# The up projection's products with both parts of x in one, its halves added afterwards, and the large sums in whole PSUM banks

## The chip, the cores and the metric

The kernel runs on one core of a Trainium2 chip. Times are device microseconds of one execution. The engines of the core are TensorE (PE), VectorE (DVE), ScalarE (ACT), GpSimd (POOL) and SyncE (SP), which here only issues DMAs. PE takes its weights from SBUF and writes to PSUM, which has eight banks of 128 partitions by 512 float32.

## The reference

A decoder trunk of two layers, batch 1, 256 positions, width 1024. In each layer four token mixers (stick-breaking, MoBA, NSA and differential attention) read one normalised input through one combined projection, their heads go through one output projection, and a squared-ReLU MLP of width 4096 follows. Cut to the layer:

```python
h = _rmsnorm(x, g_attn) @ w_in          # columns for four mixers
...
x = x + concat(heads) @ w_out
h = _rmsnorm(x, g_mlp)
x = x + square(relu(h @ w_up)) @ w_down
```

All values are float32.

## The kernel before

**Split products.** PE runs on float32r operands, which keep fewer bits than float32. Every operand of a weight product is therefore split into a high part and a rest (`whi` and `wlo`, `xh` and `xl`), and a product is the sum of three: high by high, low by high, high by low.

**Weights.** `Weights.load` brings a piece of 1 MB by a DMA on SP's queue into one of three `wraw` buffers. `Weights.part` makes the parts of each half of it: a copy on ACT gives `whi`, a subtraction on DVE `wlo` (four buffers each).

**Stages.** Per layer: `make_xT` transposes the normalised input; `attention` runs the projections group by group (`proj`: nqk, dqk, v2, mqk and others) and the mixers. `stack2` and `stack3` copy high and low parts of q and k (`qth`, `qtl`) from SBUF to SBUF by DMA into stacked tiles `s`, from which PE multiplies. `out_proj` sums the mixers' outputs (`mixh`, `mixl`) into `xs`. `mlp` transposes `xs`, and then runs 16 steps j: `up(j)` makes 256 rows of the hidden layer in one bank (two halves c2 of 128 rows by 256 positions), `down(j)` multiplies them by 256 rows of `w_down` and adds to sums that stay in PSUM over all j. In these sums the positions 0 to 127 (t=0) have two banks of 512 columns, and the positions 128 to 255 (t=1) one of 512 and two of 256 (`COLS`). The last two steps are done for t=0 first and then for t=1 (`late`).

**Order.** No instruction is issued as the code stands. All calls are recorded by a class `Order` with a clock (`at(...)`) and a price (`estimate`); a planner in the kernel then lists them by engine, takes buffers in that order, and issues them all from line 480. Fitted numbers shift the clocks: `START` for the mixers, `LOADS` for each piece's DMA, `LEADS` for the splits of its two halves, `FIRST` for the first transposes. So the order on every engine follows from tables, and a profile shows line 480 for all instructions; they are told apart by tiles.

Of the kernel before, what the change touches and what calls it, by code (L numbers as in the profile page):

```python
# [12 lines left out]
F32R = mybir.dt.float32r  # L13
# [11 lines left out]


START = {
    "sb": ((-1631.0, -246.3, -1469.7, 37.9), (-336.5, -802.8, -1167.9, 39.0)),
    "ns": ((24.7, -323.7, 51.7, 46.8), (48.1, -2091.9, 33.2, -513.6)),
    "cw": ((-1012.1,), (-1225.6,)),  # L30
    "cmp": ((-1143.8,), (-699.5,)),
    "df": ((-1505.4, -3076.6, -190.3, -1781.3), (-197.6, -1526.0, 53.3, 53.2)),
    "mb": ((-87.3, -375.0, -116.4, -375.3), (-1.8, -2266.1, -671.0, -7307.1)),
}

LOADS = (
    68.7, 29.2, 31.5, 51.3, 36.6, 20.0, 9.5, 12.4, 16.0, 18.7, 5.9, -3.0, 18.2, 25.0, 9.2, 6.3, 9.8, 11.4, -1.0,
    5.9, 21.8, 16.3, 17.8, 21.2, 19.9, 9.4, 20.0, 28.0, 19.8, 57.0, 26.1, 16.7, 48.9, 47.5, 12.4, 23.6, 0.7,
    34.2, 5.7, 44.0, 32.9, -9.7, -8.9, 50.3, 22.2, -0.2, 6.8, 5.6, 0.9, -15.7, 0.8, -1.0, 4.1, 12.3, 66.9, 11.7,
    21.0, 16.2, 19.5, 31.7, 16.4, 17.0, 2.2, 12.0, 15.5, 15.1, 15.5, 13.6, 7.0, 16.3, 10.4, 18.4, 18.9, 20.8,  # L40
    21.3, 38.5, 24.3, 35.9, 32.5, 35.0, 33.8, 38.0, 46.7, 46.1, 47.8, 42.4, -17.5, -43.3, -6.2, -47.0, -44.6,
    13.0, -98.1, 36.7, -17.0, 34.6, -186.6, -325.1, -520.8, -515.7, -829.1, -710.6, -2010.0, -2229.8,
)
LEADS = (
    (1347.0, 1199.9), (447.4, -513.5), (64.3, -1296.8), (1425.7, -228.5), (402.9, 87.1), (-2158.5, -31.4),
    (839.9, -708.1), (-442.8, 12.3), (5.0, -626.1), (457.2, -904.8), (23.6, 168.0), (245.1, -23.4), (74.1,
    15.0), (-742.0, -1243.8), (58.0, 77.0), (1958.8, 764.3), (68.0, 13.6), (2096.1, -632.8), (2366.8, 130.1),
    (885.9, 1.2), (646.0, 1.8), (12.9, -159.3), (-49.0, -121.0), (184.2, -17.1), (-126.7, -132.0), (988.3,
    399.4), (-372.6, -122.0), (-889.2, -1143.9), (-385.3, 112.3), (-169.7, -173.7), (3720.5, 160.6), (105.5,
    -789.1), (9.0, -138.6), (-21.2, -86.2), (307.3, -224.7), (1594.1, -229.4), (1624.4, 170.5), (-373.4, -90.2),  # L50
    (2213.6, -146.9), (-339.3, -784.8), (10.4, -954.9), (294.1, -57.0), (-93.3, 390.2), (152.5, 861.9), (1066.0,
    -1138.6), (123.6, 103.7), (-262.8, 1079.8), (545.5, -358.4), (167.1, 53.0), (215.8, 25.4), (237.4, 151.2),
    (2475.3, 5.0), (128.5, 166.4), (5.5, -36.6), (-395.1, -2225.0), (287.4, 385.8), (531.1, 940.7), (-329.1,
    386.5), (734.3, -564.9), (-121.7, -18.9), (564.5, -133.0), (252.0, 915.1), (39.9, 58.8), (34.0, -137.6),
    (-10.2, 275.5), (-292.3, -270.3), (184.7, 735.6), (1151.9, -34.2), (97.3, -1061.7), (-258.8, -1815.8),
    (259.4, 1814.3), (-47.6, 99.1), (1018.5, -2.8), (14.1, -3.1), (-1842.0, -958.3), (-136.1, -1227.7), (1.3,
    701.1), (585.0, -1068.1), (-1562.1, 1231.2), (24.5, 1607.1), (2827.1, 264.2), (608.5, -1576.0), (645.4,
    -597.8), (-122.1, 1895.3), (7.0, -329.3), (-340.0, -236.2), (-44.0, 156.5), (560.7, 294.5), (-130.7, 45.0),
    (420.1, -402.0), (-1157.7, -49.7), (2460.9, 615.7), (-445.7, -55.1), (-619.0, -2270.5), (-1175.0, -2091.0),
    (50.3, 974.9), (-18.5, 11.3), (299.0, 430.5), (25.8, 3068.0), (102.4, 1306.4), (511.2, 369.9), (-1495.2,  # L60
    181.7), (-385.3, -386.4), (-40.4, -107.4),
)
CW_LOAD = 41.5
STAGE = 1.2

FIRST = (-124.6, -741.4)
LAYER = 300.0
TINY = 1e-30
NEG = -1e30
# [108 lines left out]
class Order:  # L178
# [33 lines left out]
    def estimate(op, eng, method, writes, reads):  # L212
        o, n = writes[0], _columns_of(writes[0])
        if method == "dma_start":
            op.bytes = 4 * n * o.ap[0][1]
            if _space(o) == SBUF != _space(reads[0]) and "scratch" in reads[0].tensor.name and o.ap[0][1] < 64:
                op.bytes *= DMA_RATE / SLOW_RATE
            return 650.0 if _space(o) == _space(reads[0]) == SBUF else 475.0
        if eng == "PE":
# [264 lines left out]
def trunk(ctx: ExitStack, tc: tile.TileContext, x, w_in, w_out, w_up, w_down, gattn, gains, pos, cw1, cw2,  # L484
          lamv, subln, table, fnorm, eye, cst, hot, rows, out, order):
    nc = order
# [171 lines left out]

    def make_xT(src, gi=None):

        xh = ap.tile([128, 2, 8, 128], F32R, name="xh", tag="xh", bufs=1)
        xl = ap.tile([128, 2, 8, 128], F32R, name="xl", tag="xl", bufs=1)
        for t in range(2):
            if gi == 0:
                at(FIRST[t])
            for k4 in range(2):
# [11 lines left out]
                for i, k in enumerate(ks):  # L678
                    nc.vector.scalar_tensor_tensor(xl[:, t, k], p[:, i * 128:(i + 1) * 128], gn[:, gi, k:k + 1],
                                                   F(xh[:, t, k]), op0=ALU.mult, op1=ALU.subtract)  # L680
        return xh, xl


    COLS = (((0, 512), (512, 1024)), ((0, 512), (512, 768), (768, 1024)))

# [503 lines left out]
    VCs = []  # L1189

    def ps_out():
        return [[ps_acc() for _ in COLS[t]] for t in range(2)]

    def mms(acc, lhs, w, first, last, ts=(0, 1)):

        for t in ts:
            sl = slice(t * 128, (t + 1) * 128)
            for a, (c0, c1) in zip(acc[t], COLS[t]):
                o = a[:, :c1 - c0]
                for i, ((h, lo), (wh, wl)) in enumerate(zip(lhs, w)):  # L1200
                    mm(o, h[:, sl], wh[:, c0:c1], first and i == 0, False)
                    mm(o, h[:, sl], wl[:, c0:c1], False, False)
                    mm(o, lo[:, sl], wh[:, c0:c1], False, last and i == len(lhs) - 1)

    def out_proj(l, mix, clock):
        at(clock)
        acc = ps_out()
        late, ws = [], []
        order = [("sb", 0), ("ns", 2), ("df", 3), ("mb", 1)]
        for n, (name, idx) in enumerate(order):  # L1210
            w = Weights(w_out[l, idx], 2048, 2)
            m = mix[name].mix
            if n < 3:
                for i in range(2):
                    mms(acc, [m[i]], [w.part(i, clock)], n == 0 and i == 0, False)
                    clock += 2.6
            else:
                late += m
                ws += [w.part(i, clock + 2.6 * i) for i in range(2)]
                clock += 5.2  # L1220
        clock -= 5.2
        at(clock)
        mms(acc, late, ws, False, True, ts=(0,))
        at(clock, 2.6)
        mms(acc, late, ws, False, True, ts=(1,))
        at(clock, -4.0)
        for t in range(2):
            for a, (c0, c1) in zip(acc[t], COLS[t]):
                nc.vector.tensor_add(xs[:, t, c0:c1], a[:, :c1 - c0], xs[:, t, c0:c1])
        clock += 5.2  # L1230
        return clock + 5.2

    def mlp(l, clock):
        at(clock, -8.0)
        xh, xl = make_xT([xs[:, t] for t in range(2)], l + 1)
        at(clock, 10.0)
        r2 = [small(1), small(1)]
        for t in range(2):
# [2 lines left out]

        def up(j, clock):
            at(clock)
            p = ps_att()
            w = Weights(w_up[l, j], 2048, 2)
            hl = [w.part(c2, clock + 2.6 * c2) for c2 in range(2)]
            for c2, kh in (((0, 0), (1, 0), (0, 1), (1, 1)) if j == 0 else ((0, 0), (0, 1), (1, 0), (1, 1))):
                at(clock)
                hi, lo = hl[c2]
                o = p[:, c2 * 256:(c2 + 1) * 256]  # L1250
                for m, (a, x) in enumerate(((hi, xh), (lo, xh), (hi, xl))):
                    for k in range(4 * kh, 4 * kh + 4):
                        mm(o.rearrange("p (t c) -> p t c", t=2), a[:, k * 128:(k + 1) * 128], x[:, :, k], c2 == 0 and k == 0 and m == 0, k == 7 and m == 2)
                clock += 1.3
            at(clock)
            r, s = t2(), t2()
            nc.scalar.activation(r, p, AF.Relu)
            nc.vector.scalar_tensor_tensor(s, p, 0.0, r, op0=ALU.max, op1=ALU.mult)
            hh, hl = t2(F32R), t2(F32R)
            split(hh, hl, s)  # L1260
            return hh, hl
# [9 lines left out]
        for j in range(16):  # L1271
# [4 lines left out]
            at(c1)  # L1276
            if j < 14:
                for i in range(2):
                    mms(acc, lhs[i:i + 1], ws[i:i + 1], j == 0 and i == 0, False)
            else:  # L1280
                late.append((lhs, ws))
            h = nxt
        for t in range(2):
            for i, (lhs, ws) in enumerate(late):
                at(clock, 160.0 + 5.2 * t + 2.6 * i)
                mms(acc, lhs, ws, False, i == 1, ts=(t,))
        for t in range(2):
            for a, (c0, c1) in zip(acc[t], COLS[t]):
                nc.vector.scalar_tensor_tensor(xs[:, t, c0:c1], a[:, :c1 - c0], r2[t], xs[:, t, c0:c1],
                                               op0=ALU.mult, op1=ALU.add)  # L1290

    for l in range(DEPTH):
        at(l * LAYER, -12.0)
# [69 lines left out]
```

## Time and profile before

| | |
|---|---|
| median of three runs | 654.37 us (653.43 to 656.68) |
| the profiled execution | 658.14 us |
| its span, first to last instruction | 656.3 us |
| mean granted clock of PE in it | 0.990 |

The profile is one execution. Its span is what the views cut into stretches; 1.8 us lie around it. A clock of 1.00 is 2.4 GHz, 0.50 is 1.2 GHz.

### The profile page before, as it was taken

The page shows a single profiled execution, that of the slowest core. Times are in us where ns is not written, and L with a number is a line of the kernel's source. Part 1 is how long each engine was busy: PE and PEld are TensorE (multiplying, and loading weights), DVE is VectorE, ACT ScalarE, POOL GpSimd, SP SyncE. Part 2 cuts the span into 40 slices and gives each one's busy share as a digit, 9 for nine tenths or more (in the row PEclk, how much of TensorE's full clock was granted, in tenths as well). Part 3 has the DMA queues.
Part 4 walks back from the last instruction along what each step waited for, and adds up shares of the span by engine and source line. Part 5 has one row for each costly group of instructions (what it writes and reads, how often), then busy time and mean ns, then how long its engine had stood idle before and what let it go on. Part 6 is the DMA issues. An engine that isn't in the chain of part 4 may idle for free.

```text
span 656.3 us, 11070 instructions
## 1 busy us (share of the span) xinstructions
PE 632.1 (96%) x4390; PEld 570.7 (87%) x4390; DVE 413.1 (63%) x818; ACT 360.5 (55%) x675; POOL 8.1 (1%) x25
## 2 busy tenths in 40 slices
PE   5999999999999999999999999989999999999996
PEld 5988668789999999899889987877999999998995
DVE  6668479767536465554685585885865554655555
ACT  5556468567435445444364695866654454454443
POOL 1100000000000000000000000000000000000000
PEclk9999979999999999999999999998999999999999
DMA  7786935933645554457546977466245545545531
GB/s 295 276 258 183 268 157 207 275 129 129 212 174 193 193 191 148 174 193 257 180 143 209 276 256 194 194 192 205 100 177 205 202 172 193 193 160 193 193 129 64
DMA packets 26900, 127.02 MB, mean 194 GB/s; under 512 B 3880, under 2 KB 5928, under 8 KB 14048
## 3 DMA queue, kind: packets, MB, share of 16 engines
q1 hardware_dynamic: 26848, 126.32, 56.7%
q8 instruction: 34, 0.56, 0.3%
q14 instruction: 18, 0.15, 0.1%
HBM read 115.79 MB, written 3.17 MB: 181 GB/s over the span
## 4 chain that ended last, share of the span: by engine, by line
PE 77%; DMA 8%; DVE 6%; ACT 5%; SPq 2%; issue 1%; POOLq 0%; POOL 0%; ACTq 0%
PE ps L480 77%; ACT t L480 3%; DVE wlo L480 2%; DMA s<-qth 2%; DMA wraw<-in_w_in_dram 2%; SPq L480 2%; ACT whi L480 2%; DVE t L480 1%; DMA st<-parts_scratch 1%; DMA s<-qtl 1%; DMA wraw<-in_w_down_dram 1%; DVE xl L480 1%; DMA parts_scratch<-qth 1%; DVE sm L480 1%; DVE xs L480 1%
## 5 line engine op out<-in xcount | busy, mean ns | idle before, releaser
L480 DVE TENSOR_TENSOR wlo<-wraw,whi 128x1024 fp32r<-128x1024 f32 (+1 forms) x192 | 231.2, 1212 | 144.9 <-ACT whi L480 144.4
L480 ACT ACTIVATE whi<-wraw 128x1024 fp32r<-128x1024 f32 (+1 forms) x192 | 200.9, 1051 | 182.9 <-PE ps L480 143.1
L480 PE MATMUL ps<-whi,t 128*128 128x512 f32 (+1 forms) x640 | 169.1, 348 | 0.0
L480 PEld LDWEIGHTS ps<-whi,t 128*128 128x128 f32 x640 | 113.5, 189 | 16.3
L480 PE MATMUL ps<-xh,whi 128*128 128x256 f32 x768 | 122.6, 285 | 0.6 <-ACT whi L480 0.6
L480 PE MATMUL ps<-xl,whi 128*128 128x256 f32 x768 | 122.3, 284 | 0.0
L480 PE MATMUL ps<-xh,wlo 128*128 128x256 f32 x768 | 121.9, 284 | 0.0
L480 PE MATMUL ps<-wlo,t 128*128 128x512 f32 (+1 forms) x320 | 111.4, 349 | 0.6 <-DVE wlo L480 0.6
L480 PEld LDWEIGHTS ps<-xh,whi 128*128 128x128 f32 x768 | 105.0, 191 | 3.1 <-issue 1.4
L480 PEld LDWEIGHTS ps<-xl,whi 128*128 128x128 f32 x768 | 105.0, 191 | 0.3 <-issue 0.3
L480 PEld LDWEIGHTS ps<-xh,wlo 128*128 128x128 f32 x768 | 104.7, 192 | 0.4 <-issue 0.2
L480 PEld LDWEIGHTS ps<-wlo,t 128*128 128x128 f32 x320 | 60.6, 189 | 8.6 <-DVE wlo L480 0.9
L480 ACT ACTIVATE t<-ps 128x384 f32<-128x384 f32 (+3 forms) x79 | 40.0, 515 | 43.4 <-PE ps L480 43.0
L480 ACT ACTIVATE t<-t,sm 128x256 f32<-128x256 f32 (+1 forms) x110 | 47.2, 445 | 9.5 <-DVE sm L480 9.1
L480 DVE SCALAR_TENSOR_TENSOR t<-ps,t 128x512 f32<-128x512 f32 (+1 forms) x40 | 26.3, 660 | 23.7 <-ACT t L480 20.2
L480 DVE TENSOR_TENSOR t<-t,t 128x512 fp32r<-128x512 f32 (+2 forms) x44 | 27.4, 623 | 19.9 <-ACT t L480 19.2
L480 ACT ACTIVATE t<-t 128x512 fp32r<-128x512 f32 (+5 forms) x53 | 28.9, 548 | 14.6 <-DVE t L480 14.2
L480 DVE CUSTOM_DVE_ANT_0 t<-ps,Bt 128x256 f32<-128x256 f32 (+1 forms) x80 | 24.4, 352 | 10.9 <-PE ps L480 10.8
L480 PE MATMUL ps<-whi,mixh 128*128 128x512 f32 (+1 forms) x80 | 29.5, 370 | 0.0
L480 PE MATMUL ps<-wlo,mixh 128*128 128x512 f32 (+1 forms) x80 | 28.6, 358 | 0.0
L480 PE MATMUL ps<-whi,mixl 128*128 128x512 f32 (+1 forms) x80 | 28.5, 358 | 0.0
L480 PE MATMUL ps<-whi,xh 128*128 128x396 f32 (+1 forms) x64 | 20.7, 398 | 0.3 <-ACT xh L480 0.3
(143 smaller groups left out, 518.7 us busy)
## 6 DMA issues: line engine op xcount, KB each, us to landing
wraw<-in_w_up_dram SPq DMA_DIRECT2D x32, 1024.0 KB, 4.8
wraw<-in_w_down_dram SPq DMA_DIRECT2D x32, 1024.0 KB, 4.8
wraw<-in_w_in_dram SPq DMA_DIRECT2D x20, 1024.0 KB, 4.9
wraw<-in_cw_dram SPq DMA_DIRECT2D x8, 1024.0 KB, 5.3
wraw<-in_w_out_dram SPq DMA_DIRECT2D x8, 1024.0 KB, 6.7
s<-qth SPq DMA_DIRECT2D x28, 128.0 KB, 3.7
s<-qtl SPq DMA_DIRECT2D x28, 128.0 KB, 2.4
wraw<-in_w_in_dram SPq DMA_DIRECT2D x4, 792.0 KB, 5.5
```

What stands on the lines that cost most here:

```text
L480: fn(*a, **k)
```

## The change

It has four parts. In `up`, the parts of x stand in one tile `x4`, so that for each k the 256 columns of `xh` and the 256 of `xl` lie side by side; the high weights multiply all 512 in one product, and the low weights the 256 of `xh`. Each half c2 has a bank to itself, whose first 256 columns hold high by high and low by high, and the others high by low. ACT copies the latter to SBUF (`c`), DVE adds the former (`s`), and the squared ReLU is taken from `s`. In the sums, t=1 has two banks of 512 (`FULL`) except in the late part, which `finish` puts in one of these and two fresh banks of 256; the second bank is added to `xs` by itself. The planner's price for DMAs from SBUF to SBUF on up to 64 partitions rises. And all tables have new numbers.

```diff
 START = {
-    "sb": ((-1631.0, -246.3, -1469.7, 37.9), (-336.5, -802.8, -1167.9, 39.0)),
+    "sb": ((-2128.1, -135.2, -1435.8, 37.9), (-286.7, -731.7, -641.4, 39.7)),
...
 LOADS = (
-    68.7, 29.2, 31.5, 51.3, 36.6, 20.0, 9.5, 12.4, 16.0, 18.7, 5.9, -3.0, 18.2, 25.0, 9.2, 6.3, 9.8, 11.4, -1.0,
+    73.4, 61.3, 61.1, 82.6, 43.8, 72.8, 7.3, 8.2, 12.4, 12.9, 12.9, 2.7, 12.4, 54.6, 14.0, 10.8, 14.3, 8.1, 7.0,
...
-            if _space(o) == SBUF != _space(reads[0]) and "scratch" in reads[0].tensor.name and o.ap[0][1] < 64:
+            if _space(o) == SBUF and (_space(reads[0]) == SBUF or "scratch" in reads[0].tensor.name) and o.ap[0][1] <= 64:
                 op.bytes *= DMA_RATE / SLOW_RATE
...
-        xh = ap.tile([128, 2, 8, 128], F32R, name="xh", tag="xh", bufs=1)
-        xl = ap.tile([128, 2, 8, 128], F32R, name="xl", tag="xl", bufs=1)
+        x4 = ap.tile([128, 4096], F32R, name="x4", tag="x4", bufs=1)
+        if gi:
+
+            x4 = x4.rearrange("p (k m t c) -> p m t k c", k=8, m=2, t=2)
+        else:
+            x4 = x4.rearrange("p (m t k c) -> p m t k c", m=2, t=2, k=8)
+        xh, xl = x4[:, 0], x4[:, 1]
...
+    FULL = ((0, 512), (512, 1024))
...
-        return [[ps_acc() for _ in COLS[t]] for t in range(2)]
+        return [[ps_acc() for _ in FULL] for t in range(2)]
...
+    def finish(acc, late, clocks, add):
+
+
+        ends = [acc[0], [acc[1][0]] + [ps_acc() for _ in COLS[1][1:]]]
+        for t in range(2):
+            for i, (lhs, ws) in enumerate(late):
+                at(*clocks[t][i])
+                fresh = t == 1 and i == 0
+                mms([ends[t]] * 2, lhs, ws, (False, fresh, fresh), i == len(late) - 1, ts=(t,), cols=COLS[t])
+        add(acc[1][1], 1, 512, 1024)
+        for t in range(2):
+            for a, (c0, c1) in zip(ends[t], COLS[t]):
+                add(a, t, c0, c1)
...
         def up(j, clock):
             at(clock)
-            p = ps_att()
+            ps = [ps_att() for _ in range(2)]
             w = Weights(w_up[l, j], 2048, 2)
             hl = [w.part(c2, clock + 2.6 * c2) for c2 in range(2)]
+            c, s = t2(), t2()
             for c2, kh in (((0, 0), (1, 0), (0, 1), (1, 1)) if j == 0 else ((0, 0), (0, 1), (1, 0), (1, 1))):
                 at(clock)
                 hi, lo = hl[c2]
-                o = p[:, c2 * 256:(c2 + 1) * 256]
-                for m, (a, x) in enumerate(((hi, xh), (lo, xh), (hi, xl))):
-                    for k in range(4 * kh, 4 * kh + 4):
-                        mm(o.rearrange("p (t c) -> p t c", t=2), a[:, k * 128:(k + 1) * 128], x[:, :, k], c2 == 0 and k == 0 and m == 0, k == 7 and m == 2)
+                p = ps[c2]
+                ks = range(4 * kh, 4 * kh + 4)
+
+                for k in ks:
+                    mm(p, hi[:, k * 128:(k + 1) * 128], x4[:, :, :, k].rearrange("p m t c -> p (m t c)"), k == 0, False)
+                for k in ks:
+                    mm(p[:, 0:256], lo[:, k * 128:(k + 1) * 128], xh[:, :, k].rearrange("p t c -> p (t c)"), False, k == 7)
                 clock += 1.3
+                if kh:
+                    at(clock)
+                    cs = slice(c2 * 256, (c2 + 1) * 256)
+                    nc.scalar.activation(c[:, cs], p[:, 256:512], AF.Copy)
+                    nc.vector.tensor_add(s[:, cs], p[:, 0:256], c[:, cs])
             at(clock)
-            r, s = t2(), t2()
-            nc.scalar.activation(r, p, AF.Relu)
-            nc.vector.scalar_tensor_tensor(s, p, 0.0, r, op0=ALU.max, op1=ALU.mult)
+            nc.vector.scalar_tensor_tensor(s, s, 0.0, s, op0=ALU.max, op1=ALU.mult)
```

The order on PE where the MLP of layer 0 begins, before (`ident,xs` are the transposes for `xh` and `xl`, `mixh` and `mixl` the last products of `out_proj`):

```order
L480 MATMUL ps<-ident,xs 128x128 x6
L480 MATMUL ps<-whi,mixh 128x256
L480 MATMUL ps<-wlo,mixh 128x256
L480 MATMUL ps<-whi,mixl 128x256
L480 MATMUL ps<-xh,whi 128x256 x5
L480 MATMUL ps<-ident,xs 128x128 x2
L480 MATMUL ps<-xh,whi 128x256
L480 MATMUL ps<-xh,wlo 128x256 x4
L480 MATMUL ps<-xl,whi 128x256
```

The same place after the change (`x_435` is `x4`; the first weight is `whi`, with 512 columns):

```order
L480 MATMUL ps<-ident,xs 128x128 x6
L480 MATMUL ps<-whi,mixh 128x256
L480 MATMUL ps<-wlo,mixh 128x256
L480 MATMUL ps<-whi,mixl 128x256
L480 MATMUL ps<-ident,xs 128x128 x2
L480 MATMUL ps<-x_435,whi 128x512 x4
L480 MATMUL ps<-x_435,wlo 128x256 x4
```

Before, ten products with `xh` alone stood ahead of the first one that reads `xl`; now the first product of the MLP reads both.

The order on SP's queue in layer 1, where q and k of the MoBA group are stacked (`s2` from `qth` and `qtl`), before:

```order
L480 DMA wraw_1013<-in_w_out_dram 128x2048
L480 DMA wraw_1008<-in_w_out_dram 128x2048
L480 DMA wraw_1023<-in_w_out_dram 128x2048
L480 DMA wraw_1018<-in_w_out_dram 128x2048
L480 DMA s2_966<-qth_962 64x512 x2
L480 DMA s2_966<-qtl_963 64x512 x2
L480 DMA s2_967<-qth_964 64x512 x4
L480 DMA s2_968<-qtl_965 64x512 x4
L480 DMA wraw_1076<-in_w_up_dram 128x2048
```

After:

```order
L480 DMA wraw_1027<-in_w_out_dram 128x2048
L480 DMA wraw_972<-in_w_in_dram 128x2048
L480 DMA wraw_1022<-in_w_out_dram 128x2048
L480 DMA wraw_1032<-in_w_out_dram 128x2048
L480 DMA s2_981<-qth_977 64x512 x2
L480 DMA s2_981<-qtl_978 64x512 x2
L480 DMA s2_982<-qth_979 64x512 x4
L480 DMA s2_983<-qtl_980 64x512 x4
L480 DMA wraw_1037<-in_w_out_dram 128x2048
```

One of the four loads of `w_out` has moved behind the twelve copies.

The order on DVE in layer 0, where q and k of the NSA group are split (`qtl`, `nkl`) beside the tables of the position bias (`Bt`, `Bc`), before:

```order
L480 COPY Bc_86<-Bt_85 128x4x7
L480 COPY Bt_85<-t2_181 128x512
L480 TENSOR_TENSOR wlo_216<-wraw_212,whi_215 128x1024
L480 TENSOR_TENSOR qtl_195<-ps_182,qth_194 128x512
L480 TENSOR_TENSOR nkl_198<-ps_183,nkh_197 64x256 x3
```

After:

```order
L480 COPY Bc_86<-Bt_85 128x4x15
L480 COPY Bc_86<-Bt_85 128x4x7
L480 TENSOR_TENSOR qtl_194<-ps_181,qth_193 128x512
L480 TENSOR_TENSOR nkl_197<-ps_182,nkh_196 64x256 x2
L480 TENSOR_TENSOR wlo_295<-wraw_293,whi_294 128x1024
```

The `wlo` that stood between the bias tables and `qtl` now stands behind `qtl`, and one copy of `Bt` is gone from ahead of it.

## Rows read from the trace of the kernel before

**Rows 1.** Page of the profile, part 1: busy time of each engine

```profile
PE 632.1 (96%) x4390; PEld 570.7 (87%) x4390; DVE 413.1 (63%) x818; ACT 360.5 (55%) x675; POOL 8.1 (1%) x25
```

**Rows 2.** Busy time by stage, second MLP

```profile
core 0: us, PE busy (x) PEld busy (x) DVE busy (x) ACT busy (x) POOL busy (x), PEclk, DMA share, GB/s
470.00:644.00 174.00, 174.00 (x1198) 162.27 (x1198) 97.64 (x102) 82.24 (x99) 0.00 (x0) 1.00 0.50 179
```

**Rows 3.** Waits of PE: total us, times, longest

```profile
PE ps L480 <- DMA s<-qtl: 4.7, 2, 3.3
```

**Rows 4.** Timeline of PE; start, us, instruction, idle before it

```profile
60.55 0.47 PE L480 MATMUL ps<-nkh,s 128*128 128x512 f32 x1 [1.40 <-DMA s<-qtl]
...
80.89 0.39 PE L480 MATMUL ps<-wlo,xh 128*128 128x512 f32 x1
...
82.95 2.24 PE L480 MATMUL ps<-st 96*128 96x256 f32 x12 [1.67 <-DMA st<-parts_scratch]
...
444.39 0.48 PE L480 MATMUL ps<-s,s 128*128 128x256 f32 x2 [3.26 <-DMA s<-qtl]
```

**Rows 5.** Busy time and granted clock (PEclk) by stretch, columns as rows 2

```profile
58.00:100.00 42.00, 37.83 (x254) 28.07 (x253) 28.01 (x117) 26.30 (x80) 0.00 (x0) 0.92 0.66 206
...
84.00:88.00 4.00, 4.00 (x15) 3.27 (x14) 3.93 (x26) 4.00 (x19) 0.00 (x0) 0.50 1.00 416
...
445.00:450.00 5.00, 5.00 (x27) 4.72 (x26) 1.41 (x9) 2.00 (x4) 0.00 (x0) 0.66 0.64 224
```

**Rows 6.** Timeline of PE, spacing of matmuls

```profile
76.80 0.62 PE L480 MATMUL ps<-wlo,xh 128*128 128x512 f32 x2
...
199.90 0.64 PE L480 MATMUL ps<-xh,wlo 128*128 128x256 f32 x4
...
204.70 0.52 PE L480 MATMUL ps<-xl,whi 128*128 128x256 f32 x3
...
206.94 0.40 PE L480 MATMUL ps<-wlo,t 128*128 128x512 f32 x1
...
208.33 0.28 PE L480 MATMUL ps<-wlo,t 128*128 128x256 f32 x1
...
209.04 0.40 PE L480 MATMUL ps<-wlo,t 128*128 128x512 f32 x1
```

**Rows 7.** Groups of instructions by form: busy us, mean ns, idle before

```profile
L480 ACT ACTIVATE t<-ps 128x512 f32<-128x512 f32 x32 | 18.8, 591 | 31.5 <-PE ps L480 31.5
...
L480 DVE SCALAR_TENSOR_TENSOR t<-ps,t 128x512 f32<-128x512 f32 x32 | 21.9, 687 | 18.1 <-ACT t L480 18.0
...
L480 DVE TENSOR_TENSOR mixl<-ps,mixh 128x256 fp32r<-128x256 f32 x12 | 5.1, 422 | 9.9 <-ACT mixh L480 9.8
...
L480 ACT ACTIVATE mixh<-ps 128x256 fp32r<-128x256 f32 x12 | 4.6, 381 | 7.4 <-PE ps L480 7.4
```

**Rows 8.** Timeline of PE and DVE, start of the first MLP

```profile
148.69 0.82 PE L480 MATMUL ps<-ident,xs 128*128 128x128 f32 x6
...
149.74 0.90 PE L480 MATMUL ps<-xh,whi 128*128 128x256 f32 x5
...
150.31 1.63 DVE L480 SCALAR_TENSOR_TENSOR xl<-ps,gains,xh 128x128 fp32r<-128x128 f32 x6
...
151.31 0.29 PE L480 MATMUL ps<-xl,whi 128*128 128x256 f32 x1
```

**Rows 9.** Timeline of DVE and of SP's queue

```profile
32.45 2.45 SPq L480 DMA_DIRECT2D s<-qth  x4
...
35.00 2.48 SPq L480 DMA_DIRECT2D s<-qtl  x4
...
56.35 1.22 DVE L480 TENSOR_TENSOR wlo<-wraw,whi 128x1024 fp32r<-128x1024 f32 x1
...
57.48 0.68 DVE L480 TENSOR_TENSOR qtl<-ps,qth 128x512 fp32r<-128x512 f32 x1
...
434.00 1.10 SPq L480 DMA_DIRECT2D s<-qth  x2
...
440.91 2.38 SPq L480 DMA_DIRECT2D s<-qtl  x4
```

## What the change is predicted to do

> **What bounds the kernel now.** The page's busy line comes first: TensorE (PE) is busy 96% of a 656.3 us span [rows 1], VectorE (DVE) 63%, ScalarE (ACT) 55%. A mean over stages doesn't say where PE's other 4% are, so next come the windows by stage. In the second MLP PE is busy 174.00 of 174.00 us at clock 1.00, with DVE busy 97.64 and ACT 82.24 [rows 2]; the first MLP reads the same. There the time is the number of matmuls times their spacing, and nothing else. Third, the chain of waits: besides the start of the program, which the change hardly touches, PE waits for DMAs inside the attention stages [rows 3]. The timeline shows three places [rows 4]: 1.40 us at 60.55 for the stacked copies of q and k of the NSA group in layer 0, 1.67 us ahead of 82.95 for `st`, and 3.26 us at 444.39 for the stacked copies of the MoBA group in layer 1. Fourth, the granted clock. Behind the second and the third of these waits, where PE stood still for 1.7 us or more, it falls to its lower level, 1.2 of 2.4 GHz: 0.50 in the window 84 to 88, 0.92 on the mean of 58 to 100, and 0.66 in 445 to 450 [rows 5]. Time lost by it: 42 x 0.08 = 3.4 us in layer 0, 5 x 0.34 = 1.7 us in layer 1. Behind the wait of 1.40 us it doesn't fall.
>
> So three things can move the time: the price of a matmul in the MLP, the three waits for copies, and the clock behind two of them.
>
> **The merged matmuls.** By the order of instructions PE has 4223 matmuls before and 3507 after. 512 of the 716 that go are up matmuls: per `up` and c2, `hi` by `xh` and `hi` by `xl`, eight of 256 columns each, become eight of 512; 16 pairs an `up`, 32 `up`s. 204 are pairs in the sums of `out_proj` and `down`, 102 a layer. The columns stay the same, so only the price of an instruction beside its columns is saved. In the up stream 40 matmuls of 256 columns start between 199.90 and 204.70, which is 120.0 ns each; six of 512 columns between 206.94 and 208.33, 231.7 ns each [rows 6]. A pair merged saves 2 x 120.0 - 231.7 = 8.3 ns, 512 of them **4.25 us**. In the sums themselves six of 256 columns take 208.33 to 209.04, 118.3 ns each: 2 x 118.3 - 231.7 = 4.9 ns, 204 of them **1.0 us**. Bounds: the nearest quicker 512s are 18 that start between 76.80 and 80.89, 227.2 ns [rows 4, 6], so at most 12.8 ns a pair and 9.2 us in all; at least 4.9 ns everywhere, 3.5 us. I take the values of each one's own stream.
>
> The rows make the fixed part of a matmul about 13 ns at 256 columns (120.0 less 106.7 for the columns at 2.4 GHz). The Trainium skill, page "TensorE: Matmul & The Clock Gate", section "Back-to-back issue gap", gives a warm gap of columns divided by 2.4 plus about 2.5 ns. By that a merged pair would save 2.5 ns and all 716 only 1.8 us, an estimate from that page. By that rule a matmul of 256 would take 109 ns; the trace doesn't agree with its 120.0.
>
> **What the new evacuation of `up` costs.** Removed per `up`: an ACT relu of 512 columns from PSUM (0.591) and a DVE product from PSUM (0.687). Added: two ACT copies of 256 (nearest row 0.381), two DVE adds of 256 with one operand in PSUM (0.422), and the product on 512 columns in SBUF, which no row has as such; I price it like the one from PSUM, 0.687 [rows 7]. Per `up` that is ACT +0.17 and DVE +0.84, over 32 of them 5.4 and 27 us. DVE has 76 us idle in an MLP of 174 and gets 13.5 more to do [rows 2], so on the path this costs **0** while the chain from the last up matmul to the first down matmul of the same j is covered. Counting matmuls of the new order at the spacings above, PE has at least 5.3 us of other work between the two in 30 of 32 places; in the last j of each layer 2.77 us become 3.01 and 2.77. The chain is about 0.38 + 0.42 + 0.69 and a split of ACT 0.6 and DVE 0.7, some 2.8 us, and the first half's copy and add are done while the second half is multiplied. If the cover were gone, it would be the added add, 0.42 us each.
>
> The late part's three banks a layer cost one more DVE add in each `finish`, four in all; PE has the other part's matmuls to do meanwhile: 0.
>
> **The start of each MLP.** Here the merge has a price. Before, six transposes start at 148.69, then come the last `mixh`, `mixl` products, `xh` by `whi` from 149.74, two transposes, more `xh`, and the first product with `xl` is at 151.31, while DVE makes `xl` from 150.31, 0.27 us each [rows 8]: PE had some 1.8 us of work that needs `xh` alone. In the new order all of that is gone: three products and two transposes, about 0.6 us, stand between the six transposes and the first merged matmul, which needs `xl`. It would come to it at about 150.1, and `xl` is there at about 151.3: a wait of 1.2 us a layer, **+2.4**. Bounds: 0, if DVE starts `xl` earlier, and 1.9 each, the whole of the work that went.
>
> **The waits for copies.** (1) NSA, layer 0. On DVE a `wlo` of 1.22 us stands ahead of `qtl` at 57.48 [rows 9]; in the new order that `wlo` is behind it. The copies of `qtl` start 1.2 us earlier, so of the wait of 1.40 **1.2** go (0 to 1.4). (2) `st`, layer 0. By count the matmuls ahead of the first use grow from 10.27 to 10.81 us, so 0.5 of 1.67 go: **-0.5** (0 to -1.7). What is left, 1.2 us, is less than the 1.40 behind which the clock didn't fall, so all of its 3.4 us could come back; half a microsecond by count is too little to lean on, and I take none of it. (3) MoBA, layer 1. Four loads of `w_out`, 1 MB each, stand before the 12 copies on SP's queue, the last issued just ahead of them; after it three, and the fourth behind. The 12 took from 434.00 to 440.91 + 2.38 = 443.29, 9.3 us; eight in layer 0, with no load just ahead, 32.45 to 37.48, 5.0 us, so 12 would take 7.6 [rows 9]: **-1.7**; half a microsecond less cover on PE (7.67 to 7.16 by count) and an SP that is free up to half a microsecond earlier cancel. Bounds 0 (the third load now stands as close as the fourth did) and -3.3. Some 1.6 us are left, between the 1.40 with no fall of the clock and the 1.67 with one; I take half of its 1.7: **-0.8** (0 to -1.7).
>
> **Between the layers** the first product of the second half's norm stands behind a `wlo` and two adds in the new DVE order: **+0.5** (0 to +1.0). SP has 211 DMAs and POOL 30, before and after. The changed DMA price and the tables cost nothing by themselves; what they do is the order, counted above.
>
> **Sum:** -4.25 - 1.0 + 2.4 - 1.2 - 0.5 - 1.7 - 0.8 + 0.5 = -6.55 us, against the profiled execution's 658.14 (span 656.3 and 1.8 around it): 651.6. The median of the runs is 654.37, 0.57% below that execution, and takes the same share: **647.9 us**, 1.0% faster. About 0.5%, 3.3 us, is what a measurement of this kernel can tell from no change.
>
> **The rivals.**
> *All three waits go, and the clock stays up* (0.15). For it: two of the three are cut by half or more in the order, and the clock fell only behind the longer ones. Against it: `st` has only half a microsecond more. Of the 6.3 us of waits and 5.1 us of clock, 11.4, the sum has 4.2; the other 7.2 give 640.7, part of them 643.
> *A merged pair saves less* (0.04). If the fixed part of a matmul partly hides behind the columns, the least that rows show, 4.9 ns a pair in all, is 3.5 us in place of 5.25: 649.6. Against it: the two spacings stand 2 us apart, in one stretch of the MLP. The skill's rule in the section named above is this rival with a still smaller figure; by it 651.3 would follow, an estimate.
> *The refit gives back what the merge saves* (0.20). The order of all engines changes in every stage, and I have read it closely at five places. If the gains at copies (4.2) don't come, since a load still collides with them, 652.1 follows: no change. For it: bounds of nothing at each of these terms; against it, the two orders shown.
> *DVE becomes the bound in the MLP* (0.08), the side of slower. The chain of 2.8 us with two `wlo` of 1.22 queued ahead of its links comes to 5.2, as much as the least cover of 5.3. If each `up` exposes its added add, 32 x 0.42 = 13.4 us: 661. From 0.31 us per `up` on (10 us) the kernel is slower by over 0.5%; from 0.21 the gain is gone. Against it: 76 us of idle DVE.
>
> **How the numbers follow.** My forecast has 0.53, with 644.5 to 650.5 as its own range (merge 3.5 to 9, MLP starts 0 to 3.8, copies by bounds that don't all fall to one side). Faster by over 0.5% (under 651.1): 0.53 + 0.15 + 0.04 = 0.72; within 0.5%: 0.20; slower 0.08. The range reaches down to the partly gone waits and up to the refit's case with a margin: 642.5 to 653; left out are the full gain of the waits, the upper end of the refit's case and the slower case, together about 0.2.
>
> **What would show it.** Right: 512-column up matmuls about 232 ns apart between 256s at 120; PE still busy all through both MLPs but with a wait of about 1.2 us for `xl` at the start of each; the wait at the MoBA copies near 1.6 us with a clock above 0.8 behind it; the NSA wait near 0.2. Wrong: a wait of PE for `t` in the MLP (the slower rival), a new wait of over 1.7 us with a clock of 0.5 behind it in any attention stage, or 512s apart by less than 225 or more than 235 ns.

## The result and the profile after

The changed kernel takes 647.17 us (median of four runs, 645.89 to 648.43), beside 654.47 for the kernel before: a ratio of 0.988, with a 95% interval of 0.985 to 0.992. The forecast was 647.9. On a second chip the two take 649.40 (six runs) and 656.93 (23 runs), 0.990 (0.986 to 0.993). One of the 23 runs was in a slower state and is left out of the ratio. The changed kernel's profiled execution takes 648.43 us, with a span of 646.7 and a mean clock of 0.999.

The page and the waits of PE, after, answer to [rows 1, 3]:

```profile
PE 622.2 (96%) x3674; PEld 529.0 (82%) x3674; DVE 441.7 (68%) x900; ACT 358.9 (56%) x693; POOL 8.3 (1%) x25
...
PE ps L480 <- DMA s<-qtl: 2.6, 3, 1.3
...
PE ps L480 <- DVE xs L480: 1.2, 2, 0.6
...
PE ps L480 <- DVE x L480: 0.7, 2, 0.3
```

PE is again busy for 96% of a shorter span, DVE for 68% in place of 63%. The waits for stacked copies are shorter, and two small new kinds stand at the starts of the MLPs, for `xs` and for `x` (the tile `x4`).

The timeline of PE, after, at the three places of [rows 4]:

```profile
61.74 0.47 PE L480 MATMUL ps<-nkh,s 128*128 128x512 f32 x1 [0.27 <-DMA s<-qtl]
...
82.75 1.11 PE L480 MATMUL ps<-st 96*128 96x256 f32 x8 [0.16 <-issue]
...
438.86 0.47 PE L480 MATMUL ps<-s,s 128*128 128x256 f32 x2 [1.27 <-DMA s<-qtl]
```

The waits are 0.27, 0.16 and 1.27 us, where 1.40, 1.67 and 3.26 were. The windows that answer to [rows 2, 5]:

```profile
58.00:100.00 42.00, 40.03 (x289) 30.16 (x290) 31.13 (x133) 28.72 (x87) 0.00 (x0) 1.00 0.72 232
...
440.00:450.00 10.00, 10.00 (x58) 8.54 (x57) 8.28 (x37) 7.74 (x23) 0.00 (x0) 1.00 0.74 306
...
155.00:315.00 160.00, 160.00 (x813) 135.61 (x812) 101.40 (x120) 76.68 (x103) 0.00 (x0) 1.00 0.53 193
```

The clock is 1.00 behind both places where it had fallen, and inside the first MLP PE is busy 160.00 of 160.00 us while DVE has 101.40.

To see where the time went, the span is cut at landmarks of PE's timeline: its first transpose, the first product from `st`, the last transpose of `xs` in each layer (where the MLP begins), the last product of `down`, the last transpose of `xn` in layer 1, and the first product of the stacked MoBA copies in layer 1. All in microseconds, one profiled execution each; the last column is the time that the clock's stretches at half speed cost ahead of the last product:

| kernel | to st | st to MLP | MLP 0 | boundary | to MoBA | MoBA to MLP | MLP 1 | clock |
|---|---|---|---|---|---|---|---|---|
| before | 75.8 | 67.7 | 181.5 | 5.7 | 106.6 | 24.2 | 180.9 | 5.1 |
| after | 75.3 | 64.9 | 178.6 | 5.7 | 106.9 | 22.4 | 178.6 | 0 |
| after, again | 75.9 | 64.9 | 178.5 | 5.7 | 108.2 | 22.4 | 178.2 | 0 |

The MLPs give 2.9 and 2.3 us. The stretches behind `st` and behind the MoBA copies give 2.7 and 1.9, and there the clock is the difference that shows (3.4 and 1.7 us of it before, none after). The ways up to these two products, in which the waits themselves lie, are within 0.5 us of what they were, or longer.

The profiled execution of before lost more to the clock than most of its runs. Each run has its mean clock. Span times (1 - clock), averaged over the runs on the second chip, gives 4.6 us lost for the kernel before (23 runs) and 1.7 for the changed one (6 runs). That is 2.9 of a difference of 7.5 us; by this count the other 4.6 are work and waits. Both means also hold half speed behind the last product, where it delays no product (0.6 to 2.3 us in the profiles, 1.2 on the mean for either order), so each is too high by about 1 us, and their difference hardly is.

### The profile page after: what moved, and what is told of

It reads as the page before. It is cut to its first block, busy times and chain, and to the rows that moved or that the text cites. A ratio compares the mean times of both kernels' runs of the same rounds, so it can differ in the third digit from the quotient of the medians.

```text
span 646.7 us, 9744 instructions
## 1 busy us (share of the span) xinstructions
PE 622.2 (96%) x3674; PEld 529.0 (82%) x3674; DVE 441.7 (68%) x900; ACT 358.9 (56%) x693; POOL 8.3 (1%) x25
## 4 chain that ended last, share of the span: by engine, by line
PE 75%; DMA 9%; DVE 8%; ACT 5%; issue 1%; SPq 1%; POOLq 0%; POOL 0%; ACTq 0%; DVEq 0%
PE ps L480 75%; DMA wraw<-in_w_in_dram 3%; DVE wlo L480 3%; DVE t L480 2%; ACT t L480 2%; ACT whi L480 2%; DMA wraw<-in_cw_dram 2%; DVE xs L480 1%; DMA cst<-in_cst_dram 1%; DMA s<-qtl 1%; DMA wraw<-in_w_down_dram 1%; DVE x L480 1%; SPq L480 1%; DMA t<-bias_scratch 1%; ACT x L480 1%
## 5 line engine op out<-in xcount | busy, mean ns | idle before, releaser
L480 PE MATMUL ps<-x,whi 128*128 128x256 f32 (+1 forms) x1024 | 212.7, 341 | 0.7 <-DVE x L480 0.7
L480 PEld LDWEIGHTS ps<-x,whi 128*128 128x128 f32 x1024 | 153.8, 190 | 15.9 <-issue 1.2
L480 PEld LDWEIGHTS ps<-x,wlo 128*128 128x128 f32 x768 | 112.9, 190 | 12.0 <-issue 0.6
L480 PE MATMUL ps<-x,wlo 128*128 128x256 f32 x768 | 122.0, 283 | 0.1
L480 ACT ACTIVATE t<-ps 128x256 f32<-128x256 f32 (+1 forms) x109 | 44.1, 413 | 45.9 <-PE ps L480 45.1
L480 ACT ACTIVATE t<-t,sm 128x128 f32<-128x128 f32 (+1 forms) x98 | 42.2, 443 | 10.7 <-DVE sm L480 10.4
L480 DVE TENSOR_TENSOR t<-ps,t 128x256 f32<-128x256 f32 x64 | 26.7, 421 | 28.0 <-ACT t L480 27.3
L480 PE MATMUL ps<-whi,x 128*128 128x512 f32 (+1 forms) x128 | 36.0, 384 | 1.0 <-ACT x L480 1.0
L480 PEld LDWEIGHTS ps<-whi,x 128*128 128x128 f32 x128 | 23.1, 193 | 4.7 <-ACT x L480 1.5
L480 DVE SCALAR_TENSOR_TENSOR t<-t 128x512 f32<-128x512 f32 (+1 forms) x36 | 22.9, 635 | 1.0
```

The costliest lines, as they stand in the source:

```text
L480: fn(*a, **k)
```

## The experiments

Except where an experiment changes tables or the planner's price, the order is the recorded kernel's own, and only the named instructions are issued otherwise. Times of kernels that ran together on a chip are compared with each other, and ratios with the kernel before beside them.

### The merge of the up products alone

```diff
+for a recorded product o <- w, x of 512 columns:
+    matmul(o[:, 0:256], w, x[:, 0:256], start=start)
+    matmul(o[:, 256:512], w, x[:, 256:512], start=False)
-matmul(o, w, x, start=start)
```

The first expectation is that of the changed kernel, run once more as the measure; the second that of the run with this edit.

> The changed kernel once more, as the measure for the runs beside it. Both theories expect about 647 us; the profile's stages as before: first MLP about 178.6 us from its last transpose to its last down product, second the same.

> The changed kernel with each of the 512 up products of 512 columns issued as two of 256, in the same place of the same order; nothing else differs. My theory (a merged pair saves 8.3 ns, and the MLP is bound by PE): +4.25 us, about 651.4, each MLP 2.1 us longer. Rival (a matmul has hardly a price beside its columns, and the gain came from the refit): +1.3 us or less, under 648.5.

Measured: 649.40 us for the changed kernel and 653.66 with the products cut, +4.3. Of this 1.2 is clock by the count above (2.9 us lost in place of 1.7), so the times agree with the expected 4.25 in part by chance; the MLPs carry the reading. They take 180.5 and 180.2, 2.0 us more each, with no wait of PE in them but those at their starts. So the merge of the 512 pairs is worth 4.0 us in the trace, 7.9 ns each (predicted 8.3); beside the first profile, whose second MLP holds one more wait of 0.3, it is 3.5. The timeline of PE in the run with the cut, eight products of `whi` (those of lines 482 and 483 alternate, the first and the ninth row are shown):

```profile
200.54 0.28 PE L482 MATMUL ps<-x,whi 128*128 128x256 f32 x1
...
201.49 0.64 PE L485 MATMUL ps<-x,wlo 128*128 128x256 f32 x4
```

and in the changed kernel, four of 256 and then four of 512:

```profile
149.47 0.64 PE L480 MATMUL ps<-x,wlo 128*128 128x256 f32 x4
149.94 1.09 PE L480 MATMUL ps<-x,whi 128*128 128x512 f32 x4
150.86 0.64 PE L480 MATMUL ps<-x,wlo 128*128 128x256 f32 x4
```

Eight in 0.95 us are 119 ns each; four of 512 in 0.92 are 230 each. The price beside the columns is real, and the rival with hardly any (+1.3) falls.

### The full banks of the sums alone

```diff
+the products into the second bank of t=1 (columns 512 to 1024), all but the late part:
+    two of 256 in place of one of 512, as above
```

> The changed kernel with the 204 products into the second full bank of the sums issued as two of 256 again; nothing else differs. My theory (4.9 ns a pair): +1.0 us on PE, 0.4 us in each MLP. Rival (as in the up stream, 8.3 ns): +1.7 us. Too little for the times; it is read from the MLP stages of the profile.

Measured: 649.74 us, ratio 0.992 (0.989 to 0.994) where the changed kernel had 0.988 and 0.990; too little for the times, as expected. The MLPs take 180.2 and 179.6, which is 1.7 and 1.2 us more than the changed kernel's 178.5 and about 178.4: 2.9 us for the 168 pairs that lie in them, some 17 ns each. Both expectations were too small. The timeline of PE, changed kernel, a stretch with sums alone (23 products between the two rows):

```profile
279.78 0.62 PE L480 MATMUL ps<-whi,t 128*128 128x512 f32 x2
...
285.00 0.39 PE L480 MATMUL ps<-wlo,t 128*128 128x512 f32 x1
```

and with the cut (six of 256 between the first two rows, nine of 512 between the second and the third):

```profile
281.50 0.28 PE L482 MATMUL ps<-whi,t 128*128 128x256 f32 x1
...
282.22 0.40 PE L485 MATMUL ps<-whi,t 128*128 128x512 f32 x1
...
284.28 0.28 PE L482 MATMUL ps<-whi,t 128*128 128x256 f32 x1
```

Where every product has 512 columns they are 5.22 us / 23 = 227 ns apart. Beside pieces of 256 they are 2.06 / 9 = 229, and in the kernel before 231.7 [rows 6], while the 256s take 120. A pair merged saves 2 x 120 - 227 = 13 ns by itself, and a little on each of the 512s around it.

### The adds of the up halves

```diff
 nc.vector.tensor_add(s[:, cs], p[:, 0:256], c[:, cs])
+nc.vector.tensor_add(s[:, cs], p[:, 0:256], c[:, cs])    # issued twice
```

> The changed kernel with each of the 64 adds of the up halves done twice by VectorE (same result, same order): 27 us more work on VectorE, 0.84 us more per up. My theory (VectorE's queue is covered by PE's other work): no more than +1 us, and MLP stages within 0.5 us of the changed kernel's. Rival (VectorE is near to setting the pace): +0.42 us per up exposed or more, +13 us.

In a second run the add is left out (and the squared ReLU reads `c` alone):

```diff
-nc.vector.tensor_add(s[:, cs], p[:, 0:256], c[:, cs])
-nc.vector.scalar_tensor_tensor(s, s, 0.0, s, op0=ALU.max, op1=ALU.mult)
+nc.vector.scalar_tensor_tensor(s, c, 0.0, c, op0=ALU.max, op1=ALU.mult)
```

> The changed kernel without the 64 adds of the up halves: the squared ReLU is taken of the copied part alone, so high by high and low by high stay out of the result, while PE still makes them. My theory (the adds are covered): MLP stages within 0.3 us of the changed kernel's, time the same. Rival (each add is partly exposed, as doubling them cost 2 to 3 us an MLP): each MLP 1 us or more shorter.

Measured: doubled, 652.71 us (+3.3; MLPs 180.8 and 181.1, 2.3 and 2.9 more); left out, MLPs of 178.2 and 178.1, 0.3 less at most, and a ratio of 0.986 (0.982 to 0.989) beside the changed kernel's 0.990 (0.986 to 0.993). So the adds as they are cost nothing that can be measured, as predicted; but doubling them cost more than the +1 that my theory allowed, and far less than the rival's 13. (The MLPs grow by more than the time, since the way to MoBA is 2.8 us shorter in that profile than in the one beside it.) The window of the first MLP with doubled adds:

```profile
155.00:315.00 160.00, 159.47 (x802) 133.88 (x801) 112.31 (x150) 76.81 (x103) 0.00 (x0) 1.00 0.53 191
```

DVE has 112.31 of 160 us, and PE loses only half a microsecond in waits that show; the rest is products a little farther apart, 802 of them where the changed kernel has 813; why isn't shown. The room on DVE is there, but 27 us more work in it are not free.

### The start of the MLPs

The timeline of PE at the start of the first MLP, after:

```profile
146.65 0.28 PE L480 MATMUL ps<-whi,mixl 128*128 128x256 f32 x1
147.52 0.44 PE L480 MATMUL ps<-ident,xs 128*128 128x128 f32 x2 [0.59 <-DVE xs L480]
148.30 1.33 PE L480 MATMUL ps<-x,whi 128*128 128x512 f32 x4 [0.34 <-DVE x L480]
```

Against a spacing of 0.12 PE stands still for 0.75 us ahead of the last two transposes and 0.5 ahead of the first merged products, 1.25 in all, and the same in layer 1. The size is the predicted 1.2; but the larger part is a wait for the last piece of `xs`, which the products with `xh` alone had covered, and which I hadn't named. The experiment spreads the first products again, in the order of the changed kernel otherwise:

```diff
+4 products whi by xh (256 columns, c2=0)
 2 transposes of xs
+4 products whi by xh (256 columns, c2=1)
 8 products wlo by xh
+8 products whi by xl (256 columns)
-8 products whi by x4 (512 columns), ahead of the 4 and 4 of wlo by xh
```

> The changed kernel with the first 16 products of each MLP spread again: high weights by xh in 256 columns ahead of the last two transposes, high by xl in 256 columns behind the low products. My theory (PE waits about 1.2 us for xl and xs at the start of each MLP, and 16 pairs merged there give back only 0.13 us): -2.0 us, 645. Rival (the wait only moves to the next product that needs the second half of x): within 0.5 us of the changed kernel.

Measured: 647.45 us beside 649.40, -1.95, as expected; but the intervals of the ratios overlap (0.988, 0.984 to 0.991, and 0.990, 0.986 to 0.993), and the trace doesn't bear out all of it. The first MLP takes 177.3 us in place of 178.5, and the stretch ahead of it 65.2 in place of 64.9, since the last transposes now come later: 0.9 us gained. In layer 1 nothing is gained and 0.6 lost (178.5 and 22.6, for 178.2 and 22.4): the wait moved on, as the rival had it, to the product on the second half (1.11 us for `x`), since ScalarE made a later piece's `whi` ahead of that half's `xh` and waited 1.13 us for that piece to land. The rest of the difference lies mainly on the way to `st` (73.7 for 75.9), where nothing was edited. A second kernel moves that split too:

```diff
+layer 1: whi and wlo of one later up piece behind xh and xl of the second half
```

> The changed kernel with the first products of each MLP spread as in the run on the start, and in layer 1 the split of one later up piece put behind the second half's xh and xl on ScalarE and VectorE, since the product on the second half waited 1.1 us for x there. Expected: -3.0 us against the changed kernel, about 646; rival: the late split makes PE wait for that piece instead, no better than -2.

Measured: 644.79 us, ratio 0.982 (0.979 to 0.986), against 0.990 (0.986 to 0.993) for the changed kernel on its second chip: faster than both kernels. Its timeline of PE at the start of the first MLP shows no wait:

```profile
144.92 1.16 PE L504 MATMUL ps<-x,whi 128*128 128x256 f32 x4
145.92 0.38 PE L504 MATMUL ps<-ident,xs 128*128 128x128 f32 x2
```

The MLPs take 177.2 and 177.1 us, 1.3 and 1.2 less than the changed kernel's on its second chip, and the stretches ahead of them 0.2 and 0.3 more: 2.0 us are won at the two starts. In its one profile the ways to `st` (73.5) and to MoBA (106.6) are shorter too, by 2.4 and 1.6; what moved there isn't known.

### The clock

The kernel before, with products from constants while PE would wait:

```diff
+12 products of 256 columns into st's bank, ahead of the first product from st, layer 0
+24 products of 256 columns into the next bank, ahead of the first MoBA product, layer 1
```

> The kernel before with PE kept busy while it waits: 12 products of 256 columns from constants just ahead of the first st product of layer 0, 24 ahead of the first product of the stacked MoBA copies of layer 1, into the bank that the next product clears; order and data as before. Theory now (the change's gain outside the MLPs is the clock that no longer falls behind long waits): clock 1.00 behind both places, -3 to -5 us in the profile's stretches behind them, -2 to -3 in the mean of the runs. Rival (the waits themselves cost the time, and the clock falls for another reason): no change, or up to +1 us where the fill is longer than the wait.

The windows of that run:

```profile
58.00:100.00 42.00, 39.18 (x286) 30.04 (x285) 29.46 (x125) 27.47 (x86) 0.00 (x0) 1.00 0.71 224
...
445.00:450.00 5.00, 5.00 (x35) 4.50 (x33) 3.08 (x17) 3.71 (x12) 0.00 (x0) 1.00 0.46 184
```

The clock stays at 1.00 at both places, where it was 0.92 and 0.66 [rows 5]. From `st` to the MLP it is 66.0 us in place of 67.7 (a new wait of 1.52, for `t` from ScalarE, lies in it), from MoBA to the MLP 22.7 in place of 24.2. Over the runs the time lost to the clock falls from 4.6 to 1.5 us; the median falls only from 656.02 to 654.70, a ratio of 0.998 (0.995 to 1.001), which can't be told from no change. So it is shown that at these two places the standstill lets the clock fall, and that the stretches behind it get shorter when it doesn't. It is not shown that the whole time gets back what the clock gives: some 2 us of the 3.1 went elsewhere in this kernel. In its profile the ways to `st` (76.8) and to MoBA (107.0) are 1.0 and 0.4 longer and the second MLP (181.8) 0.9; whether that comes of the fill or is the spread between executions is open.

### The two orders at copies

```diff
 DVE, layer 0
-wlo of the projection
 qtl of the NSA group
+wlo of the projection
```

> The kernel before with qtl of the NSA group of layer 0 ahead of the wlo on VectorE, as in the changed kernel; nothing else differs. My predicted term: the NSA wait 1.2 us shorter and the time 1.2 us less. Rival (the next wait, for st, takes it, since st lands when it lands): NSA wait 1.2 us shorter, st wait as much longer, its clock fall no smaller, time within 0.5 us.

The timeline of PE with it, and the window:

```profile
61.60 0.50 PE L485 MATMUL ps<-nkh,s 128*128 128x512 f32 x1 [0.19 <-ACT nkh L485]
...
68.29 0.87 PE L485 MATMUL ps<-ident,t 128*128 128x128 f32 x6 [1.12 <-ACT t L485]
...
85.13 1.31 PE L485 MATMUL ps<-st 96*128 96x256 f32 x5 [2.02 <-DMA st<-parts_scratch]
...
58.00:100.00 42.00, 38.33 (x257) 28.92 (x256) 27.82 (x115) 25.82 (x77) 0.00 (x0) 0.92 0.63 197
```

The NSA wait falls from 1.40 to 0.19. Behind it a wait for `t` from ScalarE grows from 0.35 to 1.12 and the `st` wait from 1.67 to 2.02, 1.1 us together; the clock falls as before. The time ratio is 1.000 (0.998 to 1.003), which would still hold the 1.2 us of my term (0.998), so it is the trace that speaks for the rival: the microsecond that PE gained, it waited at the next two places, a third of it for `st`.

```diff
 SP, layer 1
-load of w_out (the fourth)
 12 copies for MoBA
+load of w_out (the fourth)
```

> The kernel before with the fourth load of w_out of layer 1 put behind the 12 MoBA copies on SP's queue, as in the changed kernel; nothing else differs. My predicted term (the copies no longer share with a load, 1.7 us less wait, and the clock half kept): -1.7 to -3.4 us, MoBA wait of 1.5 us or less. Rival (the wait goes to the product that needs the late load): the first MoBA product earlier, the end of the output projection not, within 0.5 us.

The timelines of PE and of ACT with it, and the time of the copies from issue to landing (median), with it and then before:

```profile
442.15 0.40 PE L487 MATMUL ps<-s,s 128*128 128x256 f32 x2
...
450.13 0.55 PE L487 MATMUL ps<-s,s 128*128 128x256 f32 x1 [6.29 <-issue]
...
447.33 1.06 ACT L487 ACTIVATE whi<-wraw 128x1024 fp32r<-128x1024 f32 x1 [7.69 <-DMA wraw<-in_w_out_dram]
...
s<-qth SPq DMA_DIRECT2D x6, 128.0 KB, 2.3
s<-qtl SPq DMA_DIRECT2D x6, 128.0 KB, 2.3
```

```profile
s<-qth SPq DMA_DIRECT2D x6, 128.0 KB, 6.5
s<-qtl SPq DMA_DIRECT2D x6, 128.0 KB, 4.6
```

The first MoBA product starts without a wait, 103.1 us after the last `xn` transpose where it was 106.6, and the copies land in 2.3 us where they took 6.5 and 4.6: they did suffer from the load. But the products of that load are next on PE, ACT waits 7.69 us for it, PE 6.29, and the clock falls behind that. The kernel is slower, 663.40 us, 1.011 (1.007 to 1.015). Neither expectation had the loss.

### The tables and the price

```diff
-START, LOADS, LEADS, FIRST of the changed kernel
+START, LOADS, LEADS, FIRST of before
```

> The changed kernel with the START, LOADS, LEADS and FIRST numbers of before. If the gain is the merge (4.25 + 1.0 less the start of the MLPs), about -3 us against the kernel before, 654 beside 657, with the attention stages as they fall out. Rival (the code's change moves all the planner's orders, and only the fitted tables bring the gain): no faster than before, 657 or more, with new long waits in attention.

```diff
-if _space(o) == SBUF and (_space(reads[0]) == SBUF or "scratch" in reads[0].tensor.name) and o.ap[0][1] <= 64:
+if _space(o) == SBUF != _space(reads[0]) and "scratch" in reads[0].tensor.name and o.ap[0][1] < 64:
```

> The changed kernel with the planner's DMA price of before, tables as fitted for the new price. If only the tables and the price together make the order that works: some us slower, 651 or more, with longer waits at copies. If the price hardly moves the order: 649, as the changed kernel.

Measured: with the old tables 667.01 us, 1.018 (1.013 to 1.023), slower than before the change; with the old price and the new tables 660.07, 1.005 (1.003 to 1.008). The timeline of PE with the old tables, and of PE with the old price, with the window of the latter:

```profile
596.02 0.80 PE L480 MATMUL ps<-wlo,t 128*128 128x512 f32 x1 [5.43 <-DVE wlo L480]
```

```profile
128.39 0.76 PE L480 MATMUL ps<-s,s 128*128 128x256 f32 x2 [3.25 <-DMA s<-qtl]
...
124.00:136.00 12.00, 8.30 (x32) 6.57 (x31) 3.57 (x17) 3.93 (x9) 0.00 (x0) 0.72 0.73 189
```

With the old tables the second MLP takes 186.0 us: a weight's split comes too late for a `down`, 5.43 us of wait in one place, and not in attention, where the rival had put the long waits. With the old price the stretch from `st` to the MLP is 75.3 us in place of 64.9, with 7.1 us of waits, the longest for stacked copies, and the clock down behind that one; the second MLP is 178.2 us there, as in the changed kernel. So the merge keeps its worth where PE doesn't wait, but the whole kernel gains only in an order that has been fitted to the changed code, as the rival had it.

## Why the prediction was right, point by point

The time (647.2 for 647.9), its sign and its mechanism in the MLP were right. Two groups of terms were wrong by about the same amount to either side, so that the sum came out better than its parts is luck. (The page counts 4390 and 3674 matmuls where the prediction has 4223 and 3507; the difference that it prices, 716, is the same.)

- **Up products**, -4.25: right, 4.0 in the trace of the run that takes the merge back. The price that the Trainium skill gives on the page "TensorE: Matmul & The Clock Gate", section "Back-to-back issue gap", columns divided by 2.4 plus 2.5 ns for a matmul by itself, would have made it 1.3 for these pairs, an estimate from that page; 227 to 233 ns for 512 columns and 117 to 120 for 256 in these runs don't agree with its 216 and 109.
- **Sums**, -1.0: mis-sized. 2.9 in the two MLPs. I took the price from a stretch where 512s and 256s alternate; with no 256s left the 512s themselves come down from 231.7 to 227 ns. The six products of 256 that I read between 208.33 and 209.04 [rows 6] are four of 256 and one of 512, which a row of the timeline merges with the last of them; the four take 0.47 us, so their 118 ns stand.
- **Adds and evacuation**, 0: right. Rows after: the ACT copy of 256 takes 373 ns (0.381 taken), the add 421 (0.422), the product in SBUF 692 (0.687).
- **Start of the MLPs**, +2.4: right in size, 2 x 1.25 in the trace, and 2.0 come back in the trace when the products are spread in both layers. Of each 1.25, 0.75 is the wait for `xs` at the transposes, not for `xl`.
- **NSA wait**, -1.2, and **`st`**, -0.5: the first wait did shrink by 1.1 us and the second by 1.5 (1.2 in the second profile), but the time to the first product from `st` moved by 0.5 at most in the profiles compared (75.8 to 75.3 and 75.9). It varies by more than that between executions: 73.5 to 76.6 over eight profiles of the changed kernel and of those with its order elsewhere, 75.8 to 78.1 over four of before and of those with its order, so a microsecond won on the way isn't ruled out. Taken alone, the first edit's gain went into the next two waits. The step that failed was adding up waits that stand behind one another.
- **MoBA**, -1.7: the wait shrank by 2.0 us (1.7 in the second profile), the time up to its product did not (106.6 to 106.9 and 108.2; 105.4 to 109.4 over the eight), as other, shorter waits stand ahead of it now: on the whole way PE waited 4.2 us before, 3.2 and 4.6 after. That the swap on SP's queue alone would help was wrong; alone it costs 7 us.
- **Clock**, -0.8: too small. 2.9 us of the difference in the runs, 5.1 in the two profiles. By the count it is the whole of what the attention stages gave. I had called the clock behind `st` possible, and left it out of the sum.
- **Between the layers**, +0.5: 0 (5.7 and 5.7).

The sum of the measured parts in runs, 4.0 + 2.9 for the merges, less 2.5 for the starts, and 2.9 of clock, is 7.3 us, which is what the medians show (7.3 and 7.5); about nothing is left for the waits for copies. The terms of the MLP in this sum rest on experiments. The 2.9 of clock is a count: filling the waits of the kernel before took 3.1 us off the same count and only 1.3 off the median, so part of the 2.9 may be waits after all.

The rival of a DVE-bound MLP is ruled out for this kernel by leaving the adds out. The rival in which the refit gives back what the merge saves was right that the waits for copies would give about nothing, and wrong on the time, since the sums and the clock gave more. What the refit is worth by itself isn't shown; without it, with the tables of before, the changed code is 11 us slower than the kernel before.

## What to carry to other kernels

A wait that was shortened here ahead of other waits gave its time to the next ones: price the last landing, not each wait. Ask of each remaining standstill whether the clock falls behind it, since cutting one long wait into shorter ones can win more by the clock than by the wait. And where a wide product replaces two narrow ones, look at its first instance, which needs all of its operand at once: the narrow ones had been cover.

## What the runs showed of the hardware

The spacing of 512-column products depends on what stands among them: 227 ns in a stretch of them alone, 229 to 233 where products of 256 are mixed in. In the fourteen profiles, from 20 us on and up to the last product, single waits of PE of up to 1.63 us left the clock at 1.00, with one exception; waits of 1.67, 1.75, 1.97, 1.99, 2.02 us and more were followed by a stretch at 0.50, with two. The exceptions are, first, in the changed kernel with the old tables, where the clock stays up behind 1.86 and 1.80 us, and then with the old price, where it falls behind 0.64 and 1.37:

```profile
204.65 0.73 PE L480 MATMUL ps<-x,wlo 128*128 128x256 f32 x4 [1.86 <-DVE wlo L480]
...
206.00:212.00 6.00, 5.71 (x26) 4.34 (x25) 2.60 (x3) 2.28 (x3) 0.00 (x0) 1.00 0.01 3
...
334.08 1.38 PE L480 MATMUL ps<-ident,xn 128*128 128x128 f32 x8 [1.80 <-DVE xn L480]
...
335.00:345.00 10.00, 9.22 (x52) 8.24 (x52) 6.39 (x11) 4.39 (x9) 1.22 (x1) 1.00 0.40 140
```

```profile
158.20 0.44 PE L480 MATMUL ps<-ident,xs 128*128 128x128 f32 x2 [0.64 <-DVE xs L480]
160.01 1.34 PE L480 MATMUL ps<-x,whi 128*128 128x512 f32 x4 [1.37 <-DVE x L480]
...
161.00:165.00 4.00, 4.00 (x16) 3.52 (x16) 3.93 (x12) 1.22 (x3) 0.00 (x0) 0.57 0.00 0
```

So the length of one wait doesn't settle it; what else does isn't shown here. With constants multiplied in part of such a wait (1.06 and 1.46 us left), the clock stayed at 1.00.
